# An encoder trunk on one core: the mLSTM's running maxima brought to all partitions by SyncE transfers instead of GpSimd broadcasts

## The chip, the cores and the metric

The kernel runs on one core of one Trainium2 chip. The metric is the device time of one execution in microseconds. Before the change the median of three runs is 901.01 us (900.82 to 901.49). The engines are called TensorE (PE in the profile, with PEld for its weight loads), VectorE (DVE), ScalarE (ACT), GpSimd (POOL) and SyncE (SP, which only issues transfers here). Each engine takes its own instructions in order, and waits on semaphores where it needs another engine's result.

## The reference

The program is a trunk of two layers over one sequence of 256 tokens of width 1024 in float32. Each layer is a half SwiGLU feed-forward, a mixer, and another half SwiGLU feed-forward, each followed by a scaled residual and a layer norm. The mixer of layer 0 is a bidirectional mLSTM with 4 heads (key width 128, value width 256); that of layer 1 is windowed attention.

```
def reference(x, ...):
    for l in range(DEPTH):
        x = layer_norm(ALPHA * x + 0.5 * swiglu(x, ffn_w_in[l, 0], ffn_w_out[l, 0]), ...)
        y = mlstm_mixer(...) if l % 2 == 0 else window_attention(...)
        x = layer_norm(ALPHA * x + y, ...)
        x = layer_norm(ALPHA * x + 0.5 * swiglu(x, ffn_w_in[l, 1], ffn_w_out[l, 1]), ...)
    return x
```

What matters of the mLSTM: each token s has an input gate i(s) and a forget gate f(s) for each head and direction. With the running sum c(t) of log sigmoid(f), a query at t weighs the key at s by exp(c(t) - c(s) + i(s) - m(t)), where m(t) is the stabiliser. Written with u(s) = i(s) - c(s) and the running maximum p(t) = max(0, max of u(s) up to t), the weight is exp(u(s) - p(t)). The output is the weighted sum of values, divided by the larger of the weighted sum of q.k (in absolute value) and exp(-m(t)). The backward direction does the same on the reversed sequence, and the two are added, normalised for each head, gated by sigmoid(o), and projected.

## The kernel before

All matmuls run in a split form: each fp32 operand is cut into a high part (rounded, on ScalarE, names ending in `_hi`) and a low part (the rest, by a subtraction on VectorE, `_lo`), and each product is three matmuls (`mm3`, line 718). The weights come from HBM in words of 128 partitions x 1024 fp32 (`raw`, `b`), 512 KB each, through SyncE's queue; some are added onto words in place by transfers from GpSimd's queue (`bring`, line 950).

The order of the work is made by a planner, the class `Book` (line 262). The program notes steps; TensorE's steps stay in the order in which they were noted, and the steps of the other engines are put in order by a simulation with costs and due times: `cost` (line 348), `latest` (line 410, due times backward from TensorE's list) and `sequence` (line 438, which picks the step that can start first, and among those the one due first). A transfer of SyncE is due LANDING + LOADING (2.2 + 1.4 us) ahead of its user; a transfer of GpSimd has a landing time from the table FEW (line 63). Transfers of SyncE are simulated in `Rings` (lines 171 to 231): for these rows, 128 x 1024 B over 16 engines, that is eight packets of 48.6 ns each, behind what is queued. Buffers are slots of a few sizes (HOMES, line 32): 16 slots "big", in which weight words and `wt` live, and 6 slots "temp", one of them for `most`. A GpSimd step of another library than the one before is planned 8 us (SWITCH) later: broadcasts are library B, plain arithmetic A.

The mLSTM stage (line 1213) takes the span from about 185 to 265 us. TensorE's order there is the string MIXES (line 52): P, S and A22 are products for v, u units of the output gate, q units of the q and k projections, g the gate matmuls, c the transposes of the gate columns, w the weights of one head, H the scores of one head, M its mix.

The step around the change runs so:
- `scans` (line 1274) works on rows: heads of the forward direction (d = 0) in partitions 0 to 3, of the backward direction (d = 1) in 36 to 39. Its last steps on VectorE are two scans with a maximum (line 1295), which write p(t) as rows of `pm`, one row of 256 tokens for each head and direction. `pm` lies in the tile `scan`.
- Line 1297: two transfers from GpSimd's queue copy the four rows of each direction into `most`, in partitions 0, 32, 64 and 96.
- `columns` (line 1303) turns u into columns (`ucol`).
- `weights(h)` (line 1315): two GpSimd broadcasts (line 1318) copy the row of head h, for each direction, to all 128 partitions of `w` (the tile `wt`). Then ScalarE makes six exponentials exp(ucol - p) of 128 x 128 (lines 1321 and 1323), and GpSimd cuts the diagonal blocks to triangles (`affine_select`, line 1325).
- `scores(h)` (line 1350): TensorE makes q.k, VectorE multiplies by `wt`, ScalarE and VectorE split the product into `a_hi` and `a_lo`.
- `mixed(h)` (line 1415): TensorE multiplies by the values, then come the division and the norm of the head, with a power on GpSimd (`hrs`, line 1399).
- At the start of the gates (line 1240) a small broadcast into `ready` makes GpSimd use its broadcast code once ahead of time.

The profile gives almost all instructions line 627, where the planner issues them, so they are told apart by the names of their tiles.

Of the kernel before, what the change touches and what calls it, by code (L numbers as in the profile page):

```python
# [11 lines left out]
F32 = mybir.dt.float32  # L12
# [8 lines left out]
S = 256  # L21
# [38 lines left out]
ISSUE = 600.0  # L60
LANDING = 2200.0
LOADING = 1400.0
FEW = {"most": 3200.0, "few": 9500.0}
SWITCH = 8000.0
SHARED = ("partition_broadcast", "affine_select", "tensor_scalar", "tensor_tensor")
ADDING = 5500.0
# [195 lines left out]
class Book:  # L262
# [147 lines left out]
    def latest(self):  # L410
# [19 lines left out]
        for s in reversed(steps):  # L430
# [3 lines left out]
            if s.name == "dma_start":  # L434
                after += ADDING + LANDING if s.kw.get("accum_op") is not None else FEW[s.outs[0].room.name] if s.engine == "POOL" else LANDING + LOADING
            s.due = min([steps[d].due for d in [*s.succ, *extra[s.n]]], default=t + 5000.0) - after

    def sequence(self):
# [55 lines left out]
        while len(given) < len(steps):  # L494
# [49 lines left out]
            if s.name == "dma_start":  # L544
                if e == "POOL" and s.kw.get("accum_op") is None:
                    s.lands = s.end + FEW[s.outs[0].room.name]
                elif loads < len(RAMP):
# [83 lines left out]
def trunk_kernel(ctx: ExitStack, tc: tile.TileContext, x, ffn_w_in, ffn_w_out, ln_g, ln_b, ml_w_in, ml_gate_b,  # L631
# [6 lines left out]
    nc = Book(tc.nc, (rooms, banks, smalls))  # L638
# [4 lines left out]
    def const(name, shape, dtype=F32):  # L643
        t = consts.tile(list(shape), dtype, name=name)
        v = nc.tile(name, shape, "const", dtype)
        v.room.real = t
        v.room.slot = 0
        return v
# [10 lines left out]
    def temp(name, n=512, dtype=F32):  # L659
        return nc.tile(name, (128, n), "temp", dtype)  # L660

    def small(name, shape):
        return nc.tile(name, shape, "small")
# [70 lines left out]
    xT = tuple(const("xT" + e, [128, 8, S], FR) for e in ("_hi", "_lo"))  # L734
    ident = const("ident", [128, 128])
    few = const("few", [128, 192])
# [476 lines left out]
    def mlstm(l, n, pending, last):  # L1213
# [6 lines left out]
        for t in range(2):  # L1220
            for p, one in zip(va[t], (1.0, 0.0)):
                nc.gpsimd.memset(p[:, :, 256:258].bitcast(F32), one)
        most = temp("most").rearrange("p (d s) -> p d s", d=2)
        ones = small("ones", (64, 1))
        nc.gpsimd.memset(ones, 1.0)

# [10 lines left out]
        pg = bank((128, S))  # L1237

        def gates():
            nc.gpsimd.partition_broadcast(small("ready", (128, 8)), xT[0][0:1, 7, 248:256].bitcast(F32))  # L1240
            nc.scalar.preload_act_table_set("natural_log_exp_and_others")
            for k in range(8):
                for f in range(2):
                    nc.tensor.matmul(pg, gwi[:, k], xT[f][:, k], start=k == f == 0, stop=k == 7 and f == 1)
            scans()
# [26 lines left out]
        cum, u, pm, ex = fe, ig, fl, fe  # L1272

        def scans():
            nc.scalar.copy(gl, pg[64:128])
            nc.vector.scalar_tensor_tensor(fa[r], pg[f_], gbias[f_], gl[f_], op0=OP.add, op1=OP.add)
            nc.vector.tensor_scalar(fm[r], fa[r], 0.0, None, op0=OP.min)
            nc.vector.scalar_tensor_tensor(fa[r], fm[r], 2.0, fa[r], op0=OP.mult, op1=OP.subtract)
            nc.scalar.activation(fe[r], fa[r], AF.Exp)
            nc.scalar.activation(fl[r], fe[r], AF.Ln, bias=1.0)  # L1280
            for d in range(2):
                nc.vector.scalar_tensor_tensor(ig[32 * d:32 * d + 32], pg[r], gbias[r], gl[r], op0=OP.add, op1=OP.add)
            nc.vector.tensor_scalar(fa[r], fe[r], 1.0, None, op0=OP.add)
            nc.vector.scalar_tensor_tensor(fa[r], fa[r], 1.0, fe[r], op0=OP.subtract, op1=OP.subtract)
            nc.vector.tensor_sub(fl[r], fa[r], fl[r])
            nc.vector.tensor_add(fm[r], fm[r], fl[r])
            for d in range(2):
                q = slice(32 * d, 32 * d + 32)
                ord_ = slice(None, None, -1) if d else A
                nc.vector.tensor_tensor_scan(cum[q, ord_], ones[r].to_broadcast([32, S]), fm[r, ord_], 0.0, op0=OP.mult, op1=OP.add)  # L1290
            nc.vector.tensor_sub(u, ig, cum)
            for d in range(2):
                q = slice(32 * d, 32 * d + 32)
                ord_ = slice(None, None, -1) if d else A
                nc.vector.tensor_tensor_scan(pm[q, ord_], ones[q].to_broadcast([32, S]), u[q, ord_], 0.0, op0=OP.mult, op1=OP.max)
            for d in range(2):
                nc.gpsimd.dma_start(most[0:128:32, d], pm[36 * d:36 * d + 4])
            nc.vector.scalar_tensor_tensor(ex, cum, -1.0, pm, op0=OP.mult, op1=OP.subtract)

        ucol = temp("ucol", 128).rearrange("p (t c) -> p t c", t=2)  # L1300
# [14 lines left out]
        def weights(h):  # L1315
            w = nc.tile("wt", (128, 2, 3, 128), "big")
            for d in range(2):
                nc.gpsimd.partition_broadcast(w[:, d, 0:2].rearrange("p b m -> p (b m)"), most[32 * h:32 * h + 1, d])
            for d, blk in ((0, 1), (1, 0)):
                c = 36 * d + h  # L1320
                nc.scalar.activation(w[:, d, 2], w[:, d, blk], AF.Exp, bias=ucol[:, 1 - blk, c:c + 1], scale=-1.0)
                for sb in range(2):
                    nc.scalar.activation(w[:, d, sb], w[:, d, sb], AF.Exp, bias=ucol[:, sb, c:c + 1], scale=-1.0)
            for d in range(2):
                nc.gpsimd.affine_select(w[:, d, 0:2], w[:, d, 0:2], pattern=[[0, 2], [1 - 2 * d, 128]],
                                        compare_op=OP.is_ge, fill=0.0, base=0, channel_multiplier=2 * d - 1)
            wt.append(w)
# [5 lines left out]
        def qk(g, m, f, k):  # L1333
# [4 lines left out]
            if f == 1 and k == 7:  # L1338
# [3 lines left out]
                else:  # L1342
                    split_evac(pair(kT, A, hs), p, 128 ** -0.5)

        todo_.update(q=[lambda i=(g, m, f, k): qk(*i) for g in range(2) for m in range(2) for f in range(2) for k in range(8)],
                     u=[lambda: gate_units(1)] * 32, p=[pending], g=[gates], c=[columns], w=[lambda h=h: weights(h) for h in range(4)], sig=[lambda: sigmoids()],
                     x1=[sums[0]], x2=[sums[1]], x3=[sums[2]], x4=[sums[3]])
        am = {}
# [267 lines left out]
    for j, (kind, l, i, n) in enumerate(stages):  # L1616
        last = j == len(stages) - 1
        bound[0] = j
        if kind == "ffn":
            pending = ffn(l, i, n, pending, last)  # L1620
        elif kind == "mlstm":
            pending = mlstm(l, n, pending, last)
        else:
            pending = attn(l, n, pending, last)
# [30 lines left out]
```

## Time and profile before

| | |
|---|---|
| median of 3 runs | 901.01 us (900.82 to 901.49) |
| profiled execution | 901.09 us |
| its span (first to last instruction) | 899.3 us |
| TensorE busy | 888.0 us |
| VectorE busy | 823.5 us |
| ScalarE busy | 656.4 us |
| GpSimd busy | 164.7 us |
| bytes moved by the 16 DMA engines | 220.07 MB |
| mean granted TensorE clock | 0.998 of full speed |

A row of the timeline has the start, the duration and the engine, then the operation, the tile written and the tiles read, the shape, and a count if several neighbours of one kind are merged (the duration is then from the first start to the last end). In brackets stands how long the engine was idle before, and whose end released it; "issue" there means that nothing the profile shows held it. A row by stretches has the length, the busy time of each engine with the number of instructions, the granted clock, the mean busy share of the DMA engines, and GB/s. In the DMA view "q0" is GpSimd's queue and "q1" SyncE's, and "under 512 B 27" counts the packets below that size. A row of waits has who waited, for whom, the total in us, how often, and the longest.

### The profile page before, as it was taken

The numbers are of one execution on the slowest core, as the hardware profiler recorded it, in microseconds if no ns is written. First come the engines' busy times: TensorE is split into PE (matmuls) and PEld (weight loads), VectorE is DVE, ScalarE is ACT, GpSimd is POOL, SyncE is SP. The second block draws the span as 40 slices with busy tenths as digits, with TensorE's granted clock in tenths as the row PEclk, the third lists the DMA queues.
The fourth block names the chain that finished last, engine by engine and source line by source line (L and its number), as shares of the span: only waits on it lengthen the run. The fifth ranks groups of instructions, "written<-read, shape, count | busy, mean of one in ns | idle before, by whom it ended". The sixth has DMA issues, their size and how long they took to land.

```text
span 899.3 us, 12678 instructions
## 1 busy us (share of the span) xinstructions
PE 888.0 (99%) x4375; PEld 742.9 (83%) x4375; DVE 823.5 (92%) x1018; ACT 656.4 (73%) x927; POOL 164.7 (18%) x201
## 2 busy tenths in 40 slices
PE   9999999999999999999999999999999999999996
PEld 7888888888988888888888888888898788888885
DVE  7999998799998999999889999997889999999974
ACT  6767677687876886776769767776788888777651
POOL 0111221222322121211011211140033221111200
PEclk9999999999999999999999999999999999999999
DMA  9997997937596989999976999999643788999931
GB/s 321 380 310 218 325 314 239 312 95 224 176 317 168 249 218 329 298 265 268 346 203 164 255 307 309 292 243 348 189 125 96 178 195 231 327 279 260 302 68 47
DMA packets 107889, 220.07 MB, mean 245 GB/s; under 512 B 7305, under 2 KB 23969, under 8 KB 107825
## 3 DMA queue, kind: packets, MB, share of 16 engines
q1 hardware_dynamic: 84144, 174.09, 54.9%
q0 software_dynamic: 23680, 45.18, 28.9%
q8 instruction: 34, 0.56, 0.2%
q14 instruction: 31, 0.25, 0.1%
HBM read 218.18 MB, written 1.05 MB: 244 GB/s over the span
## 4 chain that ended last, share of the span: by engine, by line
PE 88%; DVE 8%; issue 2%; ACT 1%; POOL 0%; DVEq 0%; POOLq 0%; ACTq 0%
PE pw L627 55%; PE py L627 33%; DVE w_lo L627 4%; DVE S L627 1%; DVE scan L627 1%; DVE pr L627 1%; DVE x L627 1%; DVE pv L627 0%; DVE sc L627 0%; ACT w_hi L627 0%; ACT sc L627 0%; DVE b L627 0%; ACT S L627 0%; DVE q_lo L627 0%; ACT pr L627 0%
## 5 line engine op out<-in xcount | busy, mean ns | idle before, releaser
L627 ACT CAST w_hi<-b 128x1024 fp32r<-128x1024 f32 x280 | 292.0, 1053 | 95.9 <-PE py L627 58.7
L627 DVE TENSOR_TENSOR w_lo<-b,w_hi 128x1024 fp32r<-128x1024 f32 x280 | 334.3, 1216 | 10.5 <-ACT w_hi L627 9.7
L627 PE MATMUL pw<-w_hi,S 128*128 128x512 f32 x640 | 207.0, 390 | 0.0
L627 DVE TENSOR_TENSOR w_lo<-raw,w_hi 128x1024 fp32r<-128x1024 f32 (+1 forms) x150 | 180.0, 1212 | 11.2 <-ACT w_hi L627 9.0
L627 POOL DMA_DIRECT2D b<-in_ffn_w_in_dram x80 | 97.1, 1229 | 502.6 <-DVE b L627 196.3
L627 ACT CAST w_hi<-raw 128x1024 fp32r<-128x1024 f32 (+1 forms) x150 | 154.2, 1041 | 36.9 <-PE py L627 21.2
L627 PE MATMUL pw<-w_hi,xT_hi 128*128 128x512 f32 (+1 forms) x400 | 157.1, 394 | 0.2 <-ACT xT_hi L627 0.2
L627 PE MATMUL pw<-w_hi,xT_lo 128*128 128x512 f32 (+1 forms) x400 | 154.2, 387 | 0.7 <-DVE xT_lo L627 0.7
L627 PE MATMUL pw<-w_lo,xT_hi 128*128 128x512 f32 (+1 forms) x400 | 153.3, 386 | 0.0
L627 PEld LDWEIGHTS pw<-w_hi,S 128*128 128x128 f32 x640 | 120.1, 188 | 24.9
L627 PE MATMUL pw<-w_lo,S 128*128 128x512 f32 x320 | 124.5, 389 | 0.0
L627 PE MATMUL py<-w_hi,h_hi 128*128 128x512 f32 x317 | 124.4, 392 | 0.0
L627 PE MATMUL py<-w_hi,h_lo 128*128 128x512 f32 x317 | 123.6, 390 | 0.0
L627 PE MATMUL py<-w_lo,h_hi 128*128 128x512 f32 x317 | 123.4, 389 | 0.0
L627 DVE TENSOR_TENSOR b<-b,b 128x1024 f32<-128x1024 f32 x74 | 90.0, 1218 | 0.7
L627 PEld LDWEIGHTS pw<-w_hi,xT_lo 128*128 128x128 f32 x400 | 75.1, 188 | 17.3 <-DVE xT_lo L627 1.7
L627 PEld LDWEIGHTS pw<-w_hi,xT_hi 128*128 128x128 f32 x400 | 75.1, 188 | 14.7 <-ACT xT_hi L627 0.8
L627 PEld LDWEIGHTS pw<-w_lo,xT_hi 128*128 128x128 f32 x400 | 75.1, 188 | 13.7
L627 PEld LDWEIGHTS pw<-w_lo,S 128*128 128x128 f32 x320 | 60.1, 188 | 12.4
L627 PEld LDWEIGHTS py<-w_hi,h_lo 128*128 128x128 f32 x317 | 59.5, 188 | 12.5
L627 PEld LDWEIGHTS py<-w_lo,h_hi 128*128 128x128 f32 x317 | 59.6, 188 | 12.0
L627 PEld LDWEIGHTS py<-w_hi,h_hi 128*128 128x128 f32 x317 | 59.5, 188 | 12.0
(212 smaller groups left out, 1125.8 us busy)
## 6 DMA issues: line engine op xcount, KB each, us to landing
b<-in_ffn_w_in_dram SPq DMA_DIRECT2D x152, 512.0 KB, 8.3
raw<-in_ffn_w_out_dram SPq DMA_DIRECT2D x88, 512.0 KB, 8.8
b<-in_ffn_w_in_dram POOLq DMA_DIRECT2D x80, 512.0 KB, 9.4
raw<-in_ffn_w_in_dram SPq DMA_DIRECT2D x36, 256.0 KB, 5.9
raw<-in_ml_w_in_dram SPq DMA_DIRECT2D x16, 512.0 KB, 6.9
raw<-in_at_w_in_dram SPq DMA_DIRECT2D x12, 512.0 KB, 9.1
b<-in_ml_w_in_dram SPq DMA_DIRECT2D x8, 512.0 KB, 8.0
raw<-in_ml_w_out_dram SPq DMA_DIRECT2D x8, 512.0 KB, 4.6
```

Source lines behind the costliest of these rows:

```text
L627: getattr(engines[s.engine], s.name)(*[real(x) for x in s.args], **{k: real(x) for k, x in s.kw.items()})
```

## The change

The running maxima no longer pass through `most`. For each head and direction SyncE issues one transfer that reads the row of `pm` in its partition, repeated 128 times by a step of zero, and writes the 128 partitions of `w`. The two copies into `most`, the eight broadcasts of GpSimd and the early broadcast into `ready` are gone, as is the tile `most` and its landing time in the planner's table. The planner orders all steps of the program anew with its costs.

```
-FEW = {"most": 3200.0, "few": 9500.0}
+FEW = {"few": 9500.0}
...
-        most = temp("most").rearrange("p (d s) -> p d s", d=2)
         ones = small("ones", (64, 1))
...
         def gates():
-            nc.gpsimd.partition_broadcast(small("ready", (128, 8)), xT[0][0:1, 7, 248:256].bitcast(F32))
             nc.scalar.preload_act_table_set("natural_log_exp_and_others")
...
-            for d in range(2):
-                nc.gpsimd.dma_start(most[0:128:32, d], pm[36 * d:36 * d + 4])
             nc.vector.scalar_tensor_tensor(ex, cum, -1.0, pm, op0=OP.mult, op1=OP.subtract)
...
         def weights(h):
             w = nc.tile("wt", (128, 2, 3, 128), "big")
             for d in range(2):
-                nc.gpsimd.partition_broadcast(w[:, d, 0:2].rearrange("p b m -> p (b m)"), most[32 * h:32 * h + 1, d])
+                nc.sync.dma_start(w[:, d, 0:2].rearrange("p b m -> p (b m)"), pm[36 * d + h:36 * d + h + 1, None].to_broadcast([1, 128, S]))
```

More of the change, by code (lines that the diff above doesn't have):

```diff
@@ L62 @@
 LOADING = 1400.0
-FEW = {"most": 3200.0, "few": 9500.0}
+FEW = {"few": 9500.0}
 SWITCH = 8000.0
@@ L1222, in mlstm @@
                 nc.gpsimd.memset(p[:, :, 256:258].bitcast(F32), one)
-        most = temp("most").rearrange("p (d s) -> p d s", d=2)
         ones = small("ones", (64, 1))
@@ L1239, in gates @@
         def gates():
-            nc.gpsimd.partition_broadcast(small("ready", (128, 8)), xT[0][0:1, 7, 248:256].bitcast(F32))
             nc.scalar.preload_act_table_set("natural_log_exp_and_others")
@@ L1295, in scans @@
                 nc.vector.tensor_tensor_scan(pm[q, ord_], ones[q].to_broadcast([32, S]), u[q, ord_], 0.0, op0=OP.mult, op1=OP.max)
-            for d in range(2):
-                nc.gpsimd.dma_start(most[0:128:32, d], pm[36 * d:36 * d + 4])
             nc.vector.scalar_tensor_tensor(ex, cum, -1.0, pm, op0=OP.mult, op1=OP.subtract)
@@ L1317, in weights @@
             for d in range(2):
-                nc.gpsimd.partition_broadcast(w[:, d, 0:2].rearrange("p b m -> p (b m)"), most[32 * h:32 * h + 1, d])
+                nc.sync.dma_start(w[:, d, 0:2].rearrange("p b m -> p (b m)"), pm[36 * d + h:36 * d + h + 1, None].to_broadcast([1, 128, S]))
             for d, blk in ((0, 1), (1, 0)):
```

## The prediction, made before the changed kernel had run

> **What bounds the kernel now.** I read the page first, then the mLSTM stage (about 185 to 265 us) by stretches, then the waits of TensorE, and then the timelines of the engines around the step that the change touches.
>
> ```profile
> span 899.3 us, 12678 instructions
> PE 888.0 (99%) x4375; PEld 742.9 (83%) x4375; DVE 823.5 (92%) x1018; ACT 656.4 (73%) x927; POOL 164.7 (18%) x201
> ...
> core 0: us, PE busy (x) PEld busy (x) DVE busy (x) ACT busy (x) POOL busy (x), PEclk, DMA share, GB/s
> 215.00:225.00 10.00, 10.00 (x74) 9.31 (x73) 9.90 (x11) 4.92 (x7) 6.47 (x6) 1.00 0.38 125
> 225.00:235.00 10.00, 9.09 (x74) 8.81 (x74) 10.00 (x14) 8.46 (x18) 3.81 (x4) 1.00 0.48 163
> 235.00:245.00 10.00, 10.00 (x86) 10.00 (x85) 9.98 (x18) 7.56 (x18) 4.68 (x6) 1.00 0.50 176
> 245.00:255.00 10.00, 10.00 (x68) 9.21 (x67) 9.29 (x17) 8.75 (x23) 2.01 (x2) 1.00 0.83 283
> 255.00:265.00 10.00, 9.55 (x55) 8.12 (x54) 9.52 (x34) 7.67 (x16) 3.36 (x4) 1.00 1.02 349
> ```
>
> TensorE is busy 99% of the span, at a granted clock of 1.00, so the kernel is bound by TensorE's list of matmuls. A change that touches no matmul can win only what TensorE waits, and can lose as much as it makes TensorE wait. In the stage of the change it waits 0.91 us (225 to 235) and 0.45 us (255 to 265). VectorE is full as well, ScalarE is not. The last column but one says that the 16 DMA engines are half empty from 215 to 245 and full from 255.
>
> ```profile
> PE pw L627 <- DVE k_lo L627: 0.9, 1, 0.9
> ...
> PE py L627 <- DVE h L627: 0.4, 1, 0.4
> ```
>
> Those are the only two waits of TensorE between 195 and 270 us: one for the low half of k, one for the last normalised head. That is all that can be won here: 0.91 + 0.45 = 1.36 us. About 0.2% (1.8 us) is what a measurement of this kernel can tell from no change.
>
> **What is removed.** GpSimd loses two copies into `most`, eight broadcasts, and the early broadcast `ready`.
>
> ```profile
> L627 POOL DMA_DIRECT2D most<-scan x2: 558/610/661, 215.7 to 216.4; - x2
> ...
> DMA to landing us min/median/max: 2.1/2.4/2.6
> ...
> 218.51 5.26 POOL L627 PARTITION_BROADCAST wt<-most  x4 [1.55 <-issue]
> ...
> 218.08 1.22 DVE L627 TENSOR_TENSOR w_lo<-b,w_hi 128x1024 fp32r<-128x1024 f32 x1
> 219.22 1.44 DVE L627 TENSOR_TENSOR w_lo<-raw,w_hi 128x1024 fp32r<-128x1024 f32 x1
> ...
> 256.77 1.40 POOL L627 TENSOR_TENSOR hrs<-hrs,few 128x2 f32<-128x2 f32 x2 [7.59 <-issue]
> ```
>
> GpSimd is busy 18%, so its own time is worth nothing. Two effects on others are. Beside the broadcasts a VectorE subtraction of the same shape takes 1.44 in place of 1.22 us; four of them lie in that stretch, so about 4 x 0.22 = 0.9 us of VectorE's time is saved, on the engine that keeps TensorE waiting at k_lo. And the first power of the head norms starts only after 7.59 us in which nothing visible holds it, the first GpSimd instruction of another kind after the broadcasts; it feeds the normalised heads behind the second wait. So both waits may go: at most the 1.36 us.
>
> **What is added.** Eight SyncE transfers (four heads, two directions). Each reads one row of 256 fp32 in one partition (36d + h) 128 times and writes 128 partitions: 128 KB. Their price per piece is the whole question, and no row shows such a transfer. Below lies the rate at which all engines together load weights, above the rate at which rows came out of neighbouring partitions, which is what the two old copies did (partitions 0 to 3, then 36 to 39). Here are three stretches of the DMA view: weight loads at 212 to 213 us, the first copy at 216.97 to 217.11, and the second at 217.50 to 217.71.
>
> ```profile
> DMA packets 200, 0.38 MB, mean 381 GB/s; under 512 B 14, under 2 KB 14, under 8 KB 200
> ...
> DMA packets 29, 0.02 MB, mean 110 GB/s; under 512 B 23, under 2 KB 26, under 8 KB 28
> ...
> q0 software_dynamic: 26, 0.00, 14.0%
> ...
> DMA packets 32, 0.01 MB, mean 25 GB/s; under 512 B 27, under 2 KB 32, under 8 KB 32
> ...
> q0 software_dynamic: 32, 0.01, 17.8%
> ```
>
> Loads go at 381 GB/s, 24 GB/s for each of 16 engines: 1 KB in 43 ns. In the second copy's stretch only five 1 KB packets (32 less 27) and 27 tiny ones move. They hold 17.8% of 16 engines for 0.21 us: 0.60 us. In the first copy's stretch three rows and 23 tiny packets hold 14.0% x 16 x 0.14 = 0.31 us; with rows at 43 ns each, a tiny one has at most (0.31 - 0.13) / 23 = 8 ns. Taken off the second stretch, the five rows still took (0.60 - 27 x 0.008) / 5 = 76 ns each. So rows that several engines read from the same four partitions at once were slowed to nearly half pace, and the group together came out at 25 GB/s, the pace of one engine. The bounds for one transfer are therefore 131,072 B / 381 GB/s = 0.34 us and 131,072 B / 25 GB/s = 5.2 us, or 128 x 43 ns = 5.5 us if a single engine had to carry it. I take 5.2 us: it comes from the only row in which the source is of this kind, and there four engines read, not sixteen.
>
> The Trainium skill, "SBUF — State Buffer", section "Door 1: the DMA port swizzle", speaks against the change in the same sense: bandwidth depends on how many of 16 ports the partitions reach, and one row reaches one. With that page's 435 GB/s over 16 ports my estimate is 27 GB/s and 4.8 us for a transfer; by it the sum below would be 14.4 us in place of 17.6, and the time 915. The 25 GB/s of the second copy agrees with it.
>
> **Who waits for them.** The planner (lines 219 to 231) counts each as eight packets of 48.6 ns, so it believes they land some 4 us after issue and orders ScalarE as before. Now the rows of the first two heads:
>
> ```profile
> 214.47 1.39 DVE L627 TENSOR_TENSOR_SCAN scan<-ones,ig 32x256 f32<-32x256 f32 x2
> ...
> 225.61 3.64 ACT L627 ACTIVATE wt<-wt,ucol 128x128 f32<-128x128 f32 x12 [1.92 <-DVE ucol L627]
> 229.16 0.57 ACT L627 ACTIVATE k_hi<-pw 128x512 fp32r<-128x512 f32 x1
> ...
> 230.46 0.68 DVE L627 SCALAR_TENSOR_TENSOR k_lo<-pw,k_hi 128x512 fp32r<-128x512 f32 x1
> ...
> 231.19 0.39 PE L627 MATMUL pw<-q_hi,k_lo 128*128 128x256 f32 x1 [0.91 <-DVE k_lo L627]
> ```
>
> The scans end at 215.9. SyncE is free then (its loads, below, pause from 211.4 to 220.7), so it can issue four transfers at once. With 2.1 us from issue to landing and 5.2 us each, one behind the other, they land at 223.2, 228.4, 233.6 and 238.8. The twelve exponentials stand in ScalarE's queue ahead of k_hi, 3.64 / 12 = 0.30 us each; the last three can start at 238.8. What is queued behind them: k_hi, v_hi, weight casts, and behind k_hi TensorE. 238.8 + 0.9 (three exponentials) + 0.57 (k_hi) + 0.68 (k_lo) = 241.0, against 231.2 now. First term: **+9.8 us**.
>
> Heads 2 and 3 come to TensorE here:
>
> ```profile
> 238.41 2.05 POOL L627 PARTITION_BROADCAST wt<-most  x2 [7.25 <-DVE a_lo L627]
> ...
> 243.03 0.96 POOL L627 PARTITION_BROADCAST wt<-most  x2 [1.24 <-DVE w_lo L627]
> ...
> 247.52 1.28 ACT L627 ACT_TABLE_LOAD   x1
> 248.82 0.64 ACT L627 ACTIVATE sg<-sg 128x512 f32<-128x512 f32 x1
> 249.93 0.83 ACT L627 CAST a_hi<-wt 128x768 fp32r<-128x768 f32 x1 [0.47 <-DVE den L627]
> ...
> 250.79 0.96 DVE L627 TENSOR_TENSOR a_lo<-wt,a_hi 128x768 fp32r<-128x768 f32 x1 [0.67 <-ACT a_hi L627]
> ...
> 252.43 0.28 PE L627 MATMUL py<-v_hi,a_hi 128*128 128x258 f32 x1
> ...
> 210.00 1.35 SPq L627 DMA_DIRECT2D raw<-in_ml_w_in_dram  x2
> ...
> 220.72 0.37 SPq L627 DMA_DIRECT2D raw<-in_ml_w_in_dram  x1
> ...
> 221.26 1.16 SPq L627 DMA_DIRECT2D raw<-in_ml_w_out_dram  x2
> 227.90 13.98 SPq L627 DMA_DIRECT2D raw<-in_ml_w_out_dram  x6
> ```
>
> After the eighth landing come three exponentials, the table load, a sigmoid, a_hi and a_lo before head 2's mix: 0.9 + 1.28 + 0.64 + 0.83 + 0.96 = 4.6 us. Two ends. If all eight transfers are issued in a row (their due times are early, and buffers came free for weight loads at 221 to 228), the eighth lands at 215.9 + 2.1 + 8 x 5.2 = 259.6 and the mix starts at 264.2 in place of 252.4: 11.8 in all, 2.0 beyond the first term. If heads 2 and 3 still wait for the buffer that a_lo frees (238.4 + 9.8 = 248.2), the eighth lands at 248.2 + 2.1 + 20.8 = 271.1, the mix starts at 275.7: 23.3 in all, 13.5 beyond. I take the middle, **+7.8 us**, and not the low end, because in that case the eight `ml_w_out` loads of the last rows stand behind 41.6 us of transfers in the same queue, and their casts stand in ScalarE's queue too.
>
> The removed stalls give back the 0.45 us at most (the 0.91 is inside the first term). Sum: 9.8 + 7.8 - 0.4 = 17.2. Later stages are planned anew but do the same work; I cost them at nothing, with TensorE's full list as cover. The profiled execution took 901.09 us (span 899.3 and 1.8 around it), the median of the runs 901.01, so both give 901.1 + 17.2 = **918 us**.
>
> One more cost bounds the top. At the start TensorE goes at half pace:
>
> ```profile
> 1.24 2.50 PE L627 MATMUL py<-zero 128*128 128x256 f32 x10 [1.24 <-DVE zero L627]
> ...
> 225.07 0.28 PE L627 MATMUL pw<-xT_hi,w_hi 128*128 128x256 f32 x1
> 225.19 0.28 PE L627 MATMUL pw<-xT_lo,w_hi 128*128 128x256 f32 x1
> ```
>
> That is 0.25 us for each matmul of 256 columns, where those at 225 us start 0.12 us apart, and it lasts until about 5.5 us: some 2 us lost. No row shows whether a pause of 8 us brings this back; between 0 and 2 x 2 us. Top: 23.3, plus 8 x 0.3 for transfers of 5.5 us, plus 4: 29.7, about 930.
>
> **Rivals.** (1) *The transfers are quick.* All engines read the same row at load pace. It decides below (225.61 + 9 x 0.30 - 215.9 - 2.1) / 4 = 2.6 us for a transfer: then ScalarE's last three exponentials find their data, nothing waits, and up to 1.36 us is won: 899.7, or up to 1 us more if head 3, whose broadcasts end at 244.0 and whose transfers would land about 245.8, uses up the margin ahead of its mix. So 899.7 to 900.7, not slower. For it: DMA is half empty there, and 381 GB/s is seen. Against it: the 76 ns. The Trainium skill, "DMA: Bandwidth & Descriptors", section "Where 436 GB/s comes from", would favour it: transfers from SBUF to SBUF are bound by the fabric's 435 GB/s, an estimate of 0.3 us each. No row shows that rate with one row as source.
>
> (2) *Half slow.* The two directions lie 36 partitions apart, and a pair of transfers could run side by side: 2.6 us each in effect. The fourth lands at 228.4, no first wait; heads 2 and 3, if issued at 238.4, land at 250.9 and the mix starts at 255.5, 3.1 us late; issued earlier, not late. So 900.7 to 903.8. Against it: the transfers share one queue, in order.
>
> (3) *It does not do what it says*, since SyncE waits in order: with the transfers placed early, weight loads stand behind the scans. SyncE idles from 211.4 to 220.7 anyway, so this alone costs nothing unless the order is otherwise changed: a few us more, within the range.
>
> **How the numbers follow.** Slow transfers 0.68; quick ones 0.18 (0.05 of it faster by over 0.2%, as the new order could add a little to the 1.36); half slow 0.12 (0.05 within 0.2%, 0.07 slower); queue trouble alone 0.02. Faster 0.05, same 0.13 + 0.05 = 0.18, slower 0.77. For 8 in 10 the range must reach down into the quick case: 899.6 to 930. The slow case alone is 912 (11.8 - 0.4 more) to 930.
>
> **What would show it.** Landing of `wt` from SyncE: 5 us and growing with each of four in a row confirms, 2.5 us refutes. ScalarE's exponentials spread over more than 10 us from the first to the twelfth, TensorE waiting about 10 us for k_lo near 230 and again before the mixes of heads 2 and 3. VectorE subtractions back to 1.22 us and the head norms' first power without 7.59 us of idle time would show the removed part right. I am wrong if the fourth transfer lands before 228.

## The result, and the profile after

The changed kernel takes 917.63 us (median of 4 runs, 916.55 to 918.31) against 901.24 us for the kernel before (median of 4, 900.82 to 901.49): a ratio of 1.0181, 95% interval 1.0164 to 1.0199. That is 16.4 us slower; the prediction on record was 918.0. The profiled execution took 917.72 us with a span of 916.0 us. The total came out as forecast; its parts did not all do so.

First the page, with the busy times, and the stage by stretches (length, busy time of PE, PEld, DVE, ACT and POOL with the number of instructions, granted clock, DMA share, GB/s).

```profile
span 916.0 us, 12686 instructions
...
PE 893.4 (98%) x4375; PEld 746.7 (82%) x4375; DVE 822.0 (90%) x1018; ACT 657.0 (72%) x927; POOL 152.1 (17%) x190
```

```profile
215.00:225.00 10.00, 10.00 (x72) 9.23 (x72) 9.85 (x14) 5.17 (x8) 0.00 (x0) 1.00 0.62 39
225.00:235.00 10.00, 6.70 (x56) 6.49 (x55) 5.84 (x7) 2.29 (x8) 0.68 (x2) 1.00 0.76 40
235.00:245.00 10.00, 1.25 (x4) 1.03 (x5) 1.28 (x2) 5.11 (x14) 1.22 (x4) 0.55 0.83 94
245.00:255.00 10.00, 10.00 (x68) 10.00 (x67) 7.24 (x11) 6.40 (x12) 2.46 (x4) 0.77 0.56 168
255.00:265.00 10.00, 9.72 (x76) 9.30 (x75) 9.63 (x19) 9.32 (x20) 1.70 (x1) 1.00 0.96 347
```

The same 4375 matmuls are there. From 225 to 245 us TensorE is busy 7.95 of 20 us, and VectorE, whose `k_lo` has to wait for ScalarE's `k_hi`, 7.12. The last two columns show why a "share" misleads: from 225 to 235 the 16 DMA engines are busy 76% of the time and move 40 GB/s, where before they were busy 48% and moved 163. They are occupied, not productive: their packets take long. The granted clock is 0.55 around the pause and 0.77 in the next stretch, although TensorE is busy all through that one.

Now who waited for whom from 195 to 275 us, TensorE first and ScalarE behind it.

```profile
PE pw L627 <- ACT k_hi L627: 12.0, 1, 12.0
PE pw L627 <- DVE k_lo L627: 0.3, 1, 0.3
PE pw L627 <- DVE den L627: 0.2, 1, 0.2
```

```profile
ACT wt L627 <- DMA wt<-scan: 13.3, 4, 7.5
ACT w_hi L627 <- DMA raw<-in_ml_w_in_dram: 2.9, 2, 2.0
```

One wait of 12 us carries nearly everything. Followed back, it is ScalarE that waits, four times, for rows that the new transfers bring (13.3 us in all). The timeline of ScalarE shows what stands in its queue ahead of k_hi, and the timeline of SyncE's queue the issues:

```profile
225.02 0.41 ACT L627 ACTIVATE wt<-wt,ucol 128x128 f32<-128x128 f32 x1
232.96 1.86 ACT L627 ACTIVATE wt<-wt,ucol 128x128 f32<-128x128 f32 x6 [7.53 <-DMA wt<-scan]
237.38 1.86 ACT L627 ACTIVATE wt<-wt,ucol 128x128 f32<-128x128 f32 x6 [2.56 <-DMA wt<-scan]
240.88 0.40 ACT L627 ACTIVATE wt<-wt,ucol 128x128 f32<-128x128 f32 x1 [1.64 <-DMA wt<-scan]
242.15 1.04 ACT L627 CAST w_hi<-raw 128x1024 fp32r<-128x1024 f32 x1 [0.87 <-DMA raw<-in_ml_w_in_dram]
243.10 0.59 ACT L627 ACTIVATE k_hi<-pw 128x512 fp32r<-128x512 f32 x1
```

```profile
216.94 17.26 SPq L627 DMA_DIRECT2D wt<-scan  x6
234.30 2.09 SPq L627 DMA_DIRECT2D raw<-in_ml_w_in_dram  x1
236.48 2.93 SPq L627 DMA_DIRECT2D wt<-scan  x2
```

Read the two together. Fourteen exponentials (1 + 6 + 6 + 1) and a weight cast stand ahead of k_hi. The last exponential is released at 240.88 by a row, the cast at 242.15 by a weight word. That word was issued at 234.30, behind six row transfers. So two chains end almost together: ScalarE's wait for rows, and a weight word that is late behind the rows. Of one pause, the profile alone can't say what each is worth; the experiments below take them apart.

The timeline of TensorE around its restart, the summary of the instructions on the tile `wt`, and the first power of the head norms on GpSimd complete the picture:

```profile
243.75 0.58 PE L627 MATMUL pw<-q_hi,k_hi 128*128 128x256 f32 x1 [12.05 <-ACT k_hi L627]
...
244.47 0.58 PE L627 MATMUL pw<-q_hi,k_lo 128*128 128x256 f32 x1
```

```profile
L627 SPq DMA_DIRECT2D wt<-scan x8: 522/2242/4808, 216.9 to 238.8; - x8
...
DMA to landing us min/median/max: 6.9/11.0/16.9
```

```profile
261.35 1.70 POOL L627 TENSOR_TENSOR hrs<-hrs,few 128x2 f32<-128x2 f32 x1 [10.86 <-DVE hrs L627]
```

A row takes 6.9 to 16.9 us from issue to landing. The first four land one behind another, at 223.9, 228.1, 232.9 and 237.4, so 4.5 us each. The last transfer was issued at 238.8 and landed 8.4 us later, at 247.2: eight transfers, 1.05 MB, in 30.3 us from the first issue, or 35 GB/s. The last line answers to the 7.59 us of "issue" that the prediction wanted gone: what this power waits for now is VectorE's work, and nothing invisible. The sought gain is there. It is buried.

Where TensorE's 16.6 us came from is seen by setting its two lists of matmuls side by side, item by item, since they are the same list. By 11 us after the start the changed kernel is 1.8 us late already, well before any changed instruction can run: x arrives half a microsecond later, and TensorE takes longer to leave its slow start. The profiled experiments below have -0.1 to 1.5 us there, so I take this as scatter and no part of the change. At the k_lo matmul (231.19 before, 244.47 after) it is 13.3 late, so the stage has cost 11.5. By 249.7 it is 15.6 late: 2.3 more with hardly a wait, from matmuls of 256 columns that start some 0.21 us apart in place of 0.12. The rest adds 1.0, and the list ends 16.6 late. The profiled execution therefore shows 14.8 us of loss from the stage on; the medians differ by 16.4, and as the other executions have no trace, where the 1.6 between them lies stays open.

### The profile page after: what moved, and what is told of

Read it like the earlier page. It is cut to its first block, busy times and chain, and to the rows that moved or that the text cites. A ratio compares the mean times of both kernels' runs of the same rounds, so it can differ in the third digit from the quotient of the medians.

```text
span 916.0 us, 12686 instructions
## 1 busy us (share of the span) xinstructions
PE 893.4 (98%) x4375; PEld 746.7 (82%) x4375; DVE 822.0 (90%) x1018; ACT 657.0 (72%) x927; POOL 152.1 (17%) x190
## 3 DMA queue, kind: packets, MB, share of 16 engines
HBM read 218.18 MB, written 1.05 MB: 239 GB/s over the span
## 4 chain that ended last, share of the span: by engine, by line
PE 87%; DVE 7%; ACT 2%; issue 2%; DMA 1%; SPq 1%; POOL 0%; DVEq 0%; ACTq 0%; POOLq 0%
PE pw L627 55%; PE py L627 32%; DVE w_lo L627 2%; DMA raw<-in_ml_w_in_dram 1%; DVE pr L627 1%; SPq L627 1%; DVE scan L627 1%; DVE x L627 1%; DVE pv L627 1%; DVE sc L627 0%; DVE S L627 0%; ACT w_hi L627 0%; DMA x<-in_x_dram 0%; ACT sc L627 0%; DVE q_lo L627 0%
## 5 line engine op out<-in xcount | busy, mean ns | idle before, releaser
L627 DVE TENSOR_TENSOR w_lo<-b,w_hi 128x1024 fp32r<-128x1024 f32 x280 | 334.5, 1217 | 11.9 <-ACT w_hi L627 11.1
L627 PEld LDWEIGHTS pw<-w_hi,S 128*128 128x128 f32 x640 | 120.2, 188 | 24.9
L627 PEld LDWEIGHTS py<-w_lo,h_hi 128*128 128x128 f32 x317 | 59.6, 188 | 12.1
```

The costliest lines, as they stand in the source:

```text
L627: getattr(engines[s.engine], s.name)(*[real(x) for x in s.args], **{k: real(x) for k, x in s.kw.items()})
```

## Experiments

The theory: the rows of one group of neighbouring partitions leave at the rate of one outlet (my word for a way out that these partitions share), about 27 GB/s, however many engines fetch them; ScalarE, which takes its steps in order, waits for them with k_hi behind it. The rivals: that transfers of this many packets are slow wherever they read; that the loss is made in SyncE's queue, where weight words stand behind the rows; that each packet has a price, so that shorter ones would be worse. All times are medians in us, each beside the kernel before on the same chip.

| run | this | before | ratio (95% interval) |
|---|---|---|---|
| spread source | 900.34 | 902.74 | 0.9978 (0.9968 to 0.9988) |
| one group of partitions | 926.38 | 901.46 | 1.0272 (1.0255 to 1.0289) |
| halves | 910.74 | 902.74 | 1.0088 (1.0069 to 1.0107) |
| aside | 928.45 | 902.74 | 1.0284 (1.0267 to 1.0301) |
| aside, free slot | 931.26 | 902.03 | 1.0323 (1.0304 to 1.0341) |
| GpSimd's queue | 913.53 | 902.03 | 1.0127 (1.0114 to 1.0141) |
| true cost in the planner | 910.67 | 902.03 | 1.0096 (1.0080 to 1.0111) |
| two hops, 16 partitions | 905.28 | 902.74 | 1.0026 (1.0017 to 1.0036) |
| two hops, 8 partitions a head | 900.78 | 902.03 | 0.9987 (0.9978 to 0.9996) |

**Is it the source?** The same destination, bytes, packet size and queue, but each transfer reads 64 partitions once instead of one partition 128 times. It takes two transfers of half the size for each of the old ones:

```
-                nc.sync.dma_start(w[:, d, 0:2]..., pm[36 * d + h:36 * d + h + 1, None].to_broadcast([1, 128, S]))
+                for r_ in range(0, 128, 64):
+                    nc.sync.dma_start(w[r_:r_ + 64, d, 0:2].rearrange("p b m -> p (b m)"), pm)
```

> The eight transfers read 64 partitions (two transfers of 64 rows for each head and direction) in place of one row 128 times; the weights of the mLSTM are therefore not the right ones, and only the time counts. Same bytes, same queue, same users. Theory (a row in one partition comes out at about 27 GB/s however many engines read it, and ScalarE waits for it in order): landing in 2.5 to 4 us, TensorE does not wait for k, 900 to 903 us. Rival A (any SyncE transfer from SBUF to SBUF in rows of 1 KB is this slow): landings up to 17 us as in the changed kernel, 915 us or more. Rival B (the loss comes from the new order and from weight loads behind 1 MB more in the queue): 910 us or more.

Measured: 900.34 us against 902.74, 2.4 us faster. The summary of the tile `wt` of this run, and the only wait of TensorE from 195 to 285 us:

```profile
L627 SPq DMA_DIRECT2D wt<-scan x16: 462/592/602, 217.2 to 227.3; - x16
...
DMA to landing us min/median/max: 1.9/2.0/4.7
```

```profile
PE py L627 <- ACT xT_hi L627: 0.3, 1, 0.3
```

The median landing is 2.0 us in place of 11.0 (for half the bytes each), an issue occupies SyncE for 0.6 us in place of up to 4.8, and the waits for k_lo and h are both gone. TensorE's list is 1.4 us late ahead of the stage and 0.1 behind it, so the stage wins 1.3 of the 1.36 us that the prediction named as all there was to win. In this profiled execution, the slowest of the ten, later stages give 1.1 us back; so the trace doesn't show where the rest of the 2.4 us comes from. With the same bytes through the same queue for the same users the whole loss is gone: the slowness lies in the source of the read.

The other direction of the same test: all eight transfers read the four partitions 0 to 3, none 36 to 39.

```
-                nc.sync.dma_start(..., pm[36 * d + h:36 * d + h + 1, None].to_broadcast([1, 128, S]))
+                nc.sync.dma_start(..., pm[(h + d) % 4:(h + d) % 4 + 1, None].to_broadcast([1, 128, S]))
```

> The changed kernel with all eight transfers reading partitions 0 to 3: the backward direction takes the forward row of the next head, so its weights are not the right ones, and only the time counts. Bytes, counts, queue and users are as in the changed kernel, where the two directions read partitions 0 to 3 and 36 to 39. If neighbouring partitions share one outlet of about 27 GB/s and partitions 0 to 3 and 36 to 39 have two: no two transfers overlap any more, eight take 8 x 4.8 = 38 us from the first issue to the last landing (30.3 in the changed kernel), 920 to 930 us. If the limit belongs to each single partition, or to the transfer itself: 29 to 31 us, and the time of the changed kernel, 915 to 919 us.

Measured: 926.38 us, 24.9 more than before on that chip, inside what the theory expected. Its timeline of ScalarE is a clock for the rows:

```profile
228.40 1.58 ACT L627 ACTIVATE wt<-wt,ucol 128x128 f32<-128x128 f32 x5 [3.28 <-DMA wt<-scan]
233.28 0.40 ACT L627 ACTIVATE wt<-wt,ucol 128x128 f32<-128x128 f32 x1 [3.30 <-DMA wt<-scan]
238.03 1.57 ACT L627 ACTIVATE wt<-wt,ucol 128x128 f32<-128x128 f32 x5 [4.35 <-DMA wt<-scan]
242.85 0.40 ACT L627 ACTIVATE wt<-wt,ucol 128x128 f32<-128x128 f32 x1 [3.25 <-DMA wt<-scan]
247.72 0.40 ACT L627 ACTIVATE wt<-wt,ucol 128x128 f32<-128x128 f32 x1 [4.47 <-DMA wt<-scan]
...
252.57 0.40 ACT L627 ACTIVATE wt<-wt,ucol 128x128 f32<-128x128 f32 x1 [0.35 <-DMA wt<-scan]
```

Each start that a row released comes 4.8 us after the one before: (252.57 - 228.40) / 5 = 4.83 us for 131,072 B, 27.1 GB/s. From the first issue at 216.6 to the last landing, just ahead of 257, are some 40 us, where the changed kernel needed 30.3. Two groups of source partitions overlapped in part, one group not at all. The Trainium skill, "SBUF — State Buffer", section "Door 1: The DMA port swizzle", puts partitions 0 to 3 on one port and 36 to 39 on another, and from its 435 GB/s over 16 ports one port has an estimated 27 GB/s; both agree with this run. That single run doesn't prove the two outlets: aside, below, the two groups didn't overlap either. The last section has a stronger sign, a rate with two groups that one group never reached.

**Is it the number or the size of packets?** Each transfer cut in two, of 128 columns each (512 B packets, twice as many):

```
-                nc.sync.dma_start(w[:, d, 0:2]..., pm[36 * d + h:36 * d + h + 1, None].to_broadcast([1, 128, S]))
+                for b_ in range(2):
+                    nc.sync.dma_start(w[:, d, b_], pm[36 * d + h:36 * d + h + 1, None, tok(b_)].to_broadcast([1, 128, 128]))
```

> Each of the eight transfers is cut in two, of 128 columns each: the same bytes from the same rows, in twice as many packets of 512 B. Theory (bytes out of the partition set the price): the last of the transfers lands about as late as in the changed kernel, 914 to 921 us. Rival C (each packet from one partition has a price of its own, whatever its size): landings take twice as long, 930 us or more.

Measured: 910.74 us. A price for each packet is refuted: twice the packets were not slower but quicker than the changed kernel (1.0088 against 1.0181). My own expectation was missed too, in the same direction. The sixteen pieces landed in 25.0 us instead of 30.3 (first issue 215.1; the last at 234.3 landed 5.8 us later), and TensorE waited 8.2 us for k_hi. The pieces overlapped better; that their size did it is not shown, for a run below with whole transfers was as quick (last section).

**What does a transfer cost if nobody waits for it?** To the kernel before, eight transfers of the same rows were added that write to HBM and that nobody reads. The planner is given a fixed early due time for them.

```
+            if s.name == "dma_start" and s.ins and s.ins[0].room.name == "scan" and not s.outs:
+                s.due = 214000.0
...
+            for h in range(4):
+                for d in range(2):
+                    nc.sync.dma_start(out[0, tok(d), 256 * h:256 * h + 256], pm[36 * d + h:36 * d + h + 1, None].to_broadcast([1, 128, S]))
```

> The kernel before with GpSimd's copies and broadcasts as they were, and beside them eight SyncE transfers of the same rows, 128 times each, to rows of the output in HBM that the end of the program overwrites; nobody waits for them. It prices the queue alone. Theory (most of the loss is ScalarE's wait in order ahead of k): the transfers take 25 to 40 us, weight loads behind them come late, but TensorE waits 0 to 6 us: 901 to 907 us. Rival B (the loss is weight loads held up behind the transfers): 911 us or more.

Measured: 928.45 us, far above what was expected. TensorE waited 24.7 us for k_hi. Somebody did wait: k_hi is written into the slot that `scan`, the source of these transfers, leaves free. (The profile puts ScalarE's 21.0 us ahead of k_hi down to a weight word, but that word landed at 255.2, after k_hi had begun at 254.24; the last of the transfers had landed just before, at 253.9. With the slot kept back, in the next run, this wait is gone.) As a test of the queue the run failed; as a measurement of the price it is clean:

```profile
L629 SPq DMA_DIRECT2D out_dram<-scan x8: 589/4043/5603, 215.5 to 238.0; - x8
...
DMA to landing us min/median/max: 7.3/16.6/18.0
```

The last one, issued at 238.0, landed at 253.9, 38.4 us after the first issue: 4.8 us each, 27.3 GB/s. Here the two directions alternate as well and still did not overlap, so two groups of partitions alone do not make transfers run side by side.

The same with the slot of `scan` kept back by 40 us in the plan, so that k_hi needn't wait for it:

```
-                r.until = max(r.until, s.lands)
+                r.until = max(r.until, s.lands + (40000.0 if r.name == "scan" else 0.0))
```

> As the run before with transfers beside (the old way on GpSimd, and eight SyncE transfers of the same rows to HBM that nobody reads), but the buffer in which the rows lie is not given on to k while the transfers read it. ScalarE's exponentials wait for nothing new; only the weight loads stand behind the transfers in SyncE's queue. If ScalarE's wait for the transfers was needed for the loss: 901 to 907 us. If the held-up weight word is enough by itself (it lands about 38 us after the scans, its cast and subtraction take 2.3 us, and TensorE wants it about 24 us after the scans): 912 to 922 us.

Measured: 931.26 us, more than either case expected, and the missed size is the lesson. Waits of ScalarE, then of TensorE:

```profile
ACT w_hi L629 <- DMA raw<-in_ml_w_in_dram: 21.0, 1, 21.0
```

```profile
PE py L629 <- ACT a_hi L629: 19.5, 1, 19.5
PE pw L629 <- ACT k_hi L629: 3.6, 1, 3.6
```

No instruction uses the added rows, and yet 29 us are lost. One weight word, issued at 242.67 behind all eight, holds up ScalarE by 21.0 us, and with it a_hi: these 19.5 us of TensorE are the queue's, which by itself is enough to lose time. The 3.6 us for k_hi are not. The two old copies into `most`, in GpSimd's queue, landed 7.8 and 11.9 us after issue, where they took 2.1 to 2.6 before; they read the same partitions as the added transfers, and with them the broadcasts and the exponentials ahead of k_hi came late. What I had called a cost of nothing is the largest loss of any run here, because all eight stood ahead of that word.

**And the rows without SyncE's queue?** The same rows from GpSimd's queue, with SyncE left to the weight words. (The packets of that queue turned out to be of 4 KB and not of 1 KB.)

```
-FEW = {"few": 9500.0}
+FEW = {"wt": 2900.0, "few": 9500.0}
...
-                nc.sync.dma_start(w[:, d, 0:2]..., pm[...].to_broadcast([1, 128, S]))
+                nc.gpsimd.dma_start(w[:, d, 0:2]..., pm[...].to_broadcast([1, 128, S]))
```

> The changed kernel with its eight transfers issued by GpSimd in place of SyncE: same rows, same bytes, another queue, so that SyncE can issue weight loads all the time. Theory (the bytes out of one row's partition set the pace, whoever issues): each transfer still takes 4 to 5 us, the exponentials still wait in order, 908 to 920 us. Rival B (weight loads behind the transfers in SyncE's queue are the loss): 900 to 905 us.

Measured: 913.53 us, 11.5 more than before. Waits of ScalarE and of TensorE:

```profile
ACT wt L627 <- DMA wt<-scan: 11.6, 5, 3.5
```

```profile
PE pw L627 <- ACT den L627: 4.3, 1, 4.3
PE pw L627 <- ACT k_hi L627: 3.9, 1, 3.9
```

ScalarE's only waits for transfers are those for rows, so this wait costs time by itself, whoever issues them. The weight words were not undisturbed for all that: the two that SyncE issued at 219.0 and 220.2 landed 11.8 and 12.1 us later. The two waits of TensorE are the two terms of the prediction in small: four transfers were issued at 215.6, the next at 244.2, when the a_lo of an earlier head had freed a buffer, and their exponentials then held up ScalarE again. The clock adds to both (last section): with it, TensorE's list fell back by 6.3 us around the second wait.

**And the queue without the wait?** The planner is told 600 ns for each packet, so 4.8 us for a row, the price found aside, and the kernel is otherwise the changed one:

```
+            if s.outs and s.outs[0].room.name == "wt":
+                each = 600.0
```

> The changed kernel, with the planner told 600 ns for each packet of these transfers in place of 48.6. Nothing else is changed; it now puts k_hi and other work ahead of the exponentials of later heads. Theory (transfers land at 25 to 30 us for all eight, and what is lost is what stands behind a waiting exponential in ScalarE's order): most comes back, 901 to 907 us, TensorE waits under 5 us for k. Rival B: the last weight words still stand behind six or eight transfers in SyncE's queue, 910 us or more.

Measured: 910.67 us, 8.6 more than before: about half of the loss comes back. ScalarE's steps now stand in an order in which the exponentials hold up nobody, and TensorE waits for k no more. Its waits from 195 to 285 us:

```profile
PE pw L629 <- ACT w_hi L629: 4.8, 1, 4.8
PE pw L629 <- DVE w_lo L629: 2.2, 2, 1.3
```

Both are weight words, but not words that came late. The casts and the word behind the longer wait:

```profile
237.90 0.37 SPq L629 DMA_DIRECT2D raw<-in_ml_w_in_dram  x1
...
258.44 1.04 ACT L629 CAST w_hi<-raw 128x1024 fp32r<-128x1024 f32 x1
...
259.54 0.80 PE L629 MATMUL pw<-w_hi,xT_hi 128*128 128x512 f32 x1 [4.84 <-ACT w_hi L629]
```

This is the last word of `ml_w_in`; it landed 4.7 us after its issue, at 242.6, and its cast began 15.9 us later, behind head 3's exponentials and the table load. So what is left of the loss was made by the order planned for ScalarE, and not by a word held up in the queue. The eight rows took 25.4 us here (first issue 215.2, last landing 240.5) and not the 38.4 us that the planner now counts for eight in a row. That it put the casts late because it expected the words late is likely, but argued: no run shows the planner's own times. A better order took the waits for k away, a price set too high made others, and what the queue alone costs the changed kernel, this run doesn't measure.

**A version that pays.** If one outlet is the limit, the rows must be spread over many partitions first. First try: every row goes to 16 partitions, and from there to 128.

```
+        most = temp("most").rearrange("p (d s) -> p d s", d=2)
...
+            for h in range(4):
+                for d in range(2):
+                    nc.sync.dma_start(most[h:128:8, d], pm[36 * d + h:36 * d + h + 1, None].to_broadcast([1, 16, S]))
...
-                nc.sync.dma_start(w[:, d, 0:2]..., pm[36 * d + h:36 * d + h + 1, None].to_broadcast([1, 128, S]))
+                nc.sync.dma_start(w[:, d, 0:2]..., most[h:128:8, d][:, None].to_broadcast([16, 8, S]))
```

> Each row first goes to 16 partitions, eight apart, and from there, each row repeated eight times, to 128; nothing is left out. Theory: the first hop moves 16 KB through one source (0.6 us), the second reads from many partitions, so all sixteen transfers land within some 6 to 8 us of the scans, and the time is 900 to 904 us. Rival A: sixteen slow transfers in place of eight, 917 us or more. Rival B: as much queued as in the changed kernel, 910 us or more.

Measured: 905.28 us. The second hop landed in 3.6 us (median), so the spreading works, but the time was above what I expected. Two transfers in a row, each planned 3.6 us ahead of its user, hurried the scans ahead on VectorE (they end at 210.0 in place of 215.9), and TensorE waited 1.4 us for a w_lo and 0.5 each for an a_hi and an a_lo. The second try has one transfer for each direction in the first hop (four rows to 8 partitions each), and due times without the allowance for weights:

```
+            if s.outs and s.outs[0].room.name in ("most", "wt"):
+                after -= LOADING
...
+        most = temp("most").rearrange("p (d s) -> p d s", d=2)
...
+            for d in range(2):
+                nc.sync.dma_start(most[0:128:4, d], pm[36 * d:36 * d + 4, None].to_broadcast([4, 8, S]))
...
-                nc.sync.dma_start(w[:, d, 0:2]..., pm[36 * d + h:36 * d + h + 1, None].to_broadcast([1, 128, S]))
+                nc.sync.dma_start(w[:, d, 0:2]..., most[32 * h:32 * h + 32:4, d][:, None].to_broadcast([8, 16, S]))
```

> Nothing left out: two transfers bring the four rows of each direction to eight partitions per head, one in each fourth partition; eight more bring them from there to all 128. The planner counts 2.2 us and not 3.6 ahead for both, so that the scans are not hurried as in the first version with two hops. Theory (rows spread over partitions come quickly, and the removed broadcasts no longer slow VectorE): no wait for k, 0.1 to 0.4% below the kernel before. Rival A (transfers inside SBUF are slow): 915 us or more. If hurried scans were not what the first version lost: 905 us as there.

Measured: 900.78 us (11 runs, 899.70 to 902.73) against 902.03 (15 runs, 901.11 to 903.60), ratio 0.9987 with an interval of 0.9978 to 0.9996. It beats the changed kernel clearly and the kernel before by 1.25 us; that is less than the 1.8 us that the prediction took for the least that can be told, and only the interval, just below 1, speaks for it. Two things were changed from the first try, and the run doesn't say which of them did it. SyncE's queue and ScalarE in its stage:

```profile
216.46 1.42 SPq L629 DMA_DIRECT2D most<-scan  x2
219.81 4.07 SPq L629 DMA_DIRECT2D wt<-most  x6
223.98 0.43 SPq L629 DMA_DIRECT2D raw<-in_ml_w_in_dram  x1
```

```profile
225.94 3.63 ACT L629 ACTIVATE wt<-wt,ucol 128x128 f32<-128x128 f32 x12 [0.99 <-DVE ucol L629]
229.76 0.60 ACT L629 ACTIVATE k_hi<-pw 128x512 fp32r<-128x512 f32 x1 [0.19 <-PE pw L629]
```

Six issues fit in 4.07 us and the weight word follows at once; the twelve exponentials wait for VectorE's ucol and not for a row. TensorE's list, 1.26 us behind that of the kernel before ahead of the stage, is level with it behind the stage.

## Why the prediction was right, and where it was not

- **What bounds the kernel, and what can be won: right.** The changed kernel lost by making TensorE wait. Of the 1.36 us that could be won at most, the spread source won 1.3 in this stage. The 7.59 us ahead of the head norms' power are gone, and VectorE's subtractions take 1.2 us without the broadcasts.
- **The price of one transfer, 5.2 us: nearly right.** Alone it is 4.8 us (27.3 GB/s aside, 27.1 from one group of partitions). In the changed kernel the first four came 4.5 us apart and the later ones overlapped in part, 30.3 / 8 = 3.8 us each over all. The row that gave the price, five rows of the old copy at 76 ns each, was a thin base, but of the right kind: the same four partitions read by several engines at once. The 381 GB/s of the weight loads came from another kind of source.
- **First term, +9.8 us: right mechanism, too small.** It measured 11.5 at the k_lo matmul. The rows of the first heads came when expected (an exponential was released at 237.38; the fourth landed at 237.4, where the prediction had 238.8). But fourteen exponentials and a weight cast stood ahead of k_hi, not twelve exponentials, and the last was released at 240.88, the cast at 242.15. I took ScalarE's order from the trace of before; the planner orders anew.
- **Second term, +7.8 us: wrong.** Beyond the restart TensorE waited 0.3 and 0.2 us. This is the step that failed: the assumption that heads 2 and 3 would be held up again on top of the first delay. All eight transfers were issued by 239.4, the last landed at 247.2, and TensorE, late by then, came to those heads after their rows. The low end, "all in a row", was the case that happened, and even its 2.0 us were not lost. With GpSimd's queue, where the second batch did wait for a buffer, the term is seen: 4.3 us of waiting, 6.3 with the clock.
- **The clock after a pause: left at a bound of 0 to 2 us for each pause, taken as zero; it was 2.3.** I kept it out of the sum, since no row showed it for a pause in the middle. Other pauses cost 1.1 to 3.6 us (last section).
- **Why the total fitted.** 11.5 + 2.3 + 1.0 = 14.8 us in place of 17.2, and 1.8 us of scatter at the start of the profiled run. The second term was too big by about what the first term, the clock and this start were too small. These 1.8 us are known of the profiled execution alone. That the median met 918 within 0.4 us is in part luck; that it was slower by more than 10 us for the reason given is not.
- **The rivals.** Quick transfers: refuted for one row as source, though just what happens with 64. Half slow: its mechanism is partly real (40 us from one group; from two 30.3 in the changed kernel, 25.4 with the true cost in the planner), but in the changed kernel far from a halving. Queue trouble: I gave it 0.02 and said that it "costs nothing unless the order is otherwise changed", because SyncE idled until 220.7. That was wrong. An idle issuer at the start says nothing on the words behind 30 us of transfers: in the result one of them is released 1.27 us later than the last exponential ahead of k_hi (242.15 and 240.88), and aside, without any user of the rows, TensorE waited 19.5 us behind one.

## What to carry to other kernels

Before a transfer copies one row to all partitions, ask where it reads: find a row of the profile that reads the same few partitions, and price the transfer by that and not by the rate of the loads; if it is slow, spread the rows over partitions of many outlets in a first hop. A slow transfer costs twice, at whoever waits for the data and in the queue in which others stand behind it, and either can be enough alone, so take both apart before choosing a cure. A sum that meets the time is no proof of its terms: check each against the trace.

## What the runs showed that was not expected

**A slow transfer holds the issuing engine.** An issue takes SyncE about 0.6 us with the spread source, and up to 4.8 us in the changed kernel (522/2242/4808 ns). Later words are then held twice, at the issue and in the DMA queue.

**A pause costs more than its length.** The granted clock by stretches, of the run with GpSimd's queue:

```profile
225.00:235.00 10.00, 6.13 (x45) 5.70 (x44) 5.31 (x6) 6.80 (x16) 1.95 (x4) 0.90 0.88 269
235.00:245.00 10.00, 10.00 (x68) 10.00 (x68) 7.79 (x12) 5.39 (x10) 0.85 (x2) 0.76 0.02 6
245.00:255.00 10.00, 7.58 (x64) 7.37 (x62) 6.02 (x13) 1.83 (x5) 1.71 (x4) 1.00 1.01 144
```

After a wait of 3.9 us TensorE, busy without a break from 235 to 245, was granted 0.76, and its list fell back by another 2.4 us there, about as much as after the 12 us wait of the changed kernel (2.3). The run of two hops with waits of 1.4, 0.5 and 0.5 us kept 1.00 in all stretches. The 3.6 us wait of the run aside with the free slot was followed by half clock too, so somewhere between 1.4 and 3.6 us of waiting lies a step. The Trainium skill, "TensorE: Matmul & The Clock Gate", section "Part 1: The HAM clock gate", has half clock after an idle window of about 3.4 us; these runs agree with that, and don't fix the figure. The price of the step is no constant: the list fell back by about a further 1.1 us after that 3.6 us wait, 1.3 after 24.7 us, 2.2 after 19.2 and 3.6 after 19.5. Read in narrow stretches, the clock stands at 0.50 for 3.41 us around the wait of 3.6, and for 6.83, 10.24 and 13.65 us around those of 3.9, 8.2 and 12.0: each a multiple of 3.41. So what a pause costs depends on where in such a step TensorE comes back, and hardly on its length.

**The same rows took 25 to 38 us.** In halves (packets of 512 B) eight rows needed 25.0 us, with the true cost in the planner 25.4 (1 KB, as in the changed kernel), in the changed kernel 30.3, and written to HBM 38.4. So the size of the packets doesn't decide it; how far the two groups of partitions ran side by side does. From 224 to 228 us hardly anything but these rows moves. First the run with the true cost, which reads two groups, then the run that reads one:

```profile
DMA packets 224, 0.21 MB, mean 54 GB/s; under 512 B 22, under 2 KB 223, under 8 KB 223
```

```profile
DMA packets 116, 0.11 MB, mean 26 GB/s; under 512 B 13, under 2 KB 116, under 8 KB 116
```

Two groups can give twice the rate of one. In the same stretch the changed kernel has 40 GB/s and the run aside, also with two groups, 28. That the engines must drift apart in the queue to use both outlets at once would explain this; it is argued only, and no run here tests it.
